# The running inverse of a triangular solver: from SBUF into two PSUM banks, with the priorities of two stages set anew

## The chip, the cores and the metric

The kernel runs on one core of a Trainium2 chip. The metric is the time of one execution on the device, in microseconds; of a kernel that is timed, the median of its runs counts. Engines are called as in the profile: PE (matrix products), DVE, ACT, POOL (GpSimd) and SP (which issues the DMAs).

## The reference

Two layers of a diffusion backbone over 512 latent tokens and 256 context tokens, width 1024. Layer 0 joins a bidirectional gated delta rule (four heads of 128) with grouped-query attention; layer 1 is a Conformer convolution; a SwiGLU follows each. What matters here is the delta rule, worked in chunks of 64 tokens, and in it the triangular system of each chunk, head and direction:

```python
def gated_delta_chunked(q, k, v, g, beta, s0, need_out):
    ...
    decay = jnp.exp(jnp.where(incl, gcum[..., :, None] - gcum[..., None, :], -jnp.inf))
    kb = kc * bc
    lower = jnp.where(strict, jnp.einsum("nbhcd,nbhsd->nbhcs", kb, kc) * decay, 0.0)
    eye = jnp.eye(DELTA_CHUNK, dtype=F32)
    rhs = jnp.concatenate([vc * bc, kb * jnp.exp(gcum)[..., None]], axis=-1)
    sol = lax.linalg.triangular_solve(lower + eye, rhs, left_side=True, lower=True, unit_diagonal=True)
    u, w = sol[..., :dv], sol[..., dv:]
    ...

def bidirectional_delta(q, k, v, g, beta, s0_fwd, s0_bwd, need_out):
    o_f, s_f = gated_delta_chunked(q, k, v, g[:, :, 0], beta[:, :, 0], s0_fwd, need_out)
    rev = lambda t: jnp.flip(t, axis=1)
    o_b, s_b = gated_delta_chunked(rev(q), rev(k), rev(v), rev(g[:, :, 1]), rev(beta[:, :, 1]), s0_bwd, need_out)
```

The kernel doesn't solve against the right sides. It inverts the 32x32 blocks on the diagonal, and the next stage makes u and w from the inverses with matrix products.

## The kernel before

The work runs in four stages, each planned when the program is built: the inputs; the heads; delta rule with attention; and the tail (output projection, SwiGLU, Conformer, SwiGLU). A stage is a list of operations, each with one or more engines on which it may run and a cost for each ("ways"), with operations that it depends on, and with buffers that it takes and gives back. `Plan.run` (L62 to 124) sets them in order: again and again it takes, of all that are ready, the one with the least start time on its model, less a weight times the length of the path behind it plus a bias. The biases are tables by name, and by name and engine (`BIAS1` for the heads, `BIAS` for delta rule with attention, L134 and L135). So a table settles which engine does what and in which order each engine's instructions stand; on the chip each engine then works through its list in that order, waiting where an operand or a buffer isn't there.

The heads' stage (`plan_heads`, L590) runs until about 246 us. All 8 banks of PSUM are one pool there, "pp", of which an operation takes one bank.

- A convolution is made of matmuls in four parts (L204 to L206: three products for each of 8 blocks, as the fp32 inputs are split into a high and a low part, `whi` and `wlo`, the latter by L573 on DVE or GpSimd, from `weights`). Its bank `ps_in` is then read by taps (L653, DVE, tile `cv`), by turns for keys, values and queries.
- For attention queries, the rows of a product are normed (L956, `qn`) and turned by position ("rope": L573, tiles `qr`, `kkr`, `rt`).
- `solver(d)`, once for each of two directions (L1045 to L1100), loads the strictly lower blocks into `blk` and identity into `xi`: each has 32x32 elements on 96 partitions (four loads of 24) in SBUF, and comes from a pool "b4" of four. There are 31 steps j. `row_mul` (L1075) makes the outer product of the column of `blk` under the diagonal and the row j of `xi`, into `tm`; `row_sub` (L1079) takes it off the rows below. Each step has (31 - j)(j + 1) elements per partition, 31 at the ends, 256 in the middle, 5,456 in all. A step needs the one before, and all run on DVE; the two directions lie beside each other in its list, so that one fills the other's gaps. Then `turned` makes a transposed copy into `blk` (L564, ACT or GpSimd), and `x_out` (L1094) has four DMAs write `xi`, and four the transposed copy, to DRAM (`xblk`).
- `gate` (L1135 ff.) makes silu of a product on ACT (L1147, tile `zz`, a pool "dd" of two), times a gain on DVE or GpSimd (L573), and a DMA to DRAM (L1153, `zimg`).
- `keys64` turns keys (L1027) and makes `kst` of them (L564 and L1038). `query` sums squares on ACT (L1117, `junk`).

The next stage clears its tiles first (L1359, from `masks`, on ACT here; they are issued by the program's order behind ACT's last work of the stage before, or amid it) and loads the inverses: L1380, `xu<-xblk`. Its first DVE work is `qd<-qr`. All DMAs of these places stand in SP's one list: an issue that waits for its data holds up those behind it.

Of the kernel before, what the change touches and what calls it, by code (L numbers as in the profile page):

```python
# [151 lines left out]
def kernel(ctx: ExitStack, tc: tile.TileContext, I: dict, out: bass.AP, dbg=None):  # L152
    nc = tc.nc
    V, S, G, E, SP = nc.vector, nc.scalar, nc.gpsimd, nc.tensor, nc.sync
# [11 lines left out]
    def bc(ap, axis, shape):  # L166
        return ap.unsqueeze(axis).to_broadcast(shape)
# [134 lines left out]
    with ExitStack() as st:  # L302
# [10 lines left out]
        def copy_on(e, dst, src):  # L313
            {"ACT": S.copy, "DVE": V.tensor_copy, "Pool": G.tensor_copy}[e](dst, src)
# [262 lines left out]
    pp = pool(p1, "pp", 8, space=PSUM)  # L577
# [11 lines left out]
    def bank(n, *shape):  # L589
        return pp.tile([P] + list(shape), F32, tag="pp", name=n)  # L590

    def plan_heads(op):
# [3 lines left out]
        def after(*names):  # L596
            return tuple(last[n] for n in names if n in last)
# [175 lines left out]
        a = op({"DVE": 0.25}, g13, (a,))  # L773
# [274 lines left out]
        def solver(d):  # L1048
            s = {}

            def ld_blk():
                s["blk"] = pj.tile([96, 32, 32], F32, tag="b4", name="blk", bufs=4)
                for b in range(4):
                    src = nimg[d][32 * b : 32 * b + 32, :, :, 32 * b : 32 * b + 32].rearrange("r c h q -> (c h) r q")
                    SP.dma_start(s["blk"][b * NB : (b + 1) * NB], src)

            def ld_eye():
                s["xi"] = pj.tile([96, 32, 32], F32, tag="b4", name="xi", bufs=4)
                SP.dma_start(s["xi"].rearrange("p r q -> p (r q)"), I["eye32"].partition_broadcast(96))

            a = op({"SP": 2.2}, ld_blk, nst[d], seq=after("b4"), lat=DLAT, take=("b4",))
            b = op({"SP": 1.1}, ld_eye, (), seq=(a,), lat=DLAT, take=("b4",))
            a = op({}, None, (a, b))
            for j in range(31):
                m = 31 - j

                def step(j=j, m=m):
                    t = {}

                    def row_mul():  # L1070
                        blk, xi = s["blk"], s["xi"]
# [3 lines left out]
                        V.tensor_tensor(t["tv"], bc(col, 2, (96, m, j + 1)), bc(xi[:, j, : j + 1], 1, (96, m, j + 1)), ALU.mult)  # L1075

                    def row_sub():
                        xi = s["xi"]
                        V.tensor_tensor(xi[:, j + 1 :, : j + 1], xi[:, j + 1 :, : j + 1], t["tv"], ALU.subtract)  # L1079

                    return row_mul, row_sub

                for f in step():
                    a = op({"DVE": 0.07 + m * (j + 1) / 960.0}, f, (a,))

            def turned(e):
                s["xj"] = s["blk"]
                copy_on(e, s["xj"], s["xi"].rearrange("p r q -> p q r"))

            def x_out(w):  # L1090
                def f():
                    t_ = s["xi"] if w == d else s["xj"]
                    for b in range(4):
                        SP.dma_start(xblk[d][w, 32 * b : 32 * b + 32].rearrange("r c h q -> (c h) r q"), t_[b * NB : (b + 1) * NB])  # L1094
# [1368 lines left out]
```

## Time and profile before

| what | value |
|---|---|
| median of 3 runs | 1409.06 us (1408.97 to 1411.34) |
| the profiled execution: its own time | 1409.85 us |
| its span | 1408.1 us |
| mean granted clock of PE | 0.973 |
| busy: PE, DVE, ACT, POOL | 1339.5 (95%), 870.8 (62%), 477.1 (34%), 233.2 us (17%) |
| heads' stage before the solver, 60 to 158.5 us | PE 90.16, DVE 87.80, ACT 55.47, POOL 66.82 |
| delta rule with attention, 246.6 to 412 us | PE 162.09, DVE 141.32 of 165.4 |

The times in the rows are those of one execution, from its span's start. Busy time is what an engine spent on instructions, and the share is that of the whole span; in a window, it is read against the window's length. In the timeline, rows of one kind that follow one another are one row with a count (x2); its length runs from the first one's start to the last one's end, and neighbours overlap by some 0.06 us, since an instruction starts before the one ahead of it has drained.

### The profile page before, as it was taken

The numbers are of one execution on the slowest core, as the hardware profiler recorded it, in microseconds if no ns is written. First come the engines' busy times: TensorE is split into PE (matmuls) and PEld (weight loads), VectorE is DVE, ScalarE is ACT, GpSimd is POOL, SyncE is SP. The second block draws the span as 40 slices with busy tenths as digits, with TensorE's granted clock in tenths as the row PEclk, the third lists the DMA queues.
The fourth block names the chain that finished last, engine by engine and source line by source line (L and its number), as shares of the span: only waits on it lengthen the run. The fifth ranks groups of instructions, "written<-read, shape, count | busy, mean of one in ns | idle before, by whom it ended". The sixth has DMA issues, their size and how long they took to land.

```text
span 1408.1 us, 19059 instructions
## 1 busy us (share of the span) xinstructions
PE 1339.5 (95%) x7267; PEld 1125.3 (80%) x7267; DVE 870.8 (62%) x1634; ACT 477.1 (34%) x1003; POOL 233.2 (17%) x272
## 2 busy tenths in 40 slices
PE   6999986999999999999999989997999999999998
PEld 4888876788978988888888768886788888888886
DVE  3689898789886765565578636549574333343233
ACT  6656533577652411111100145112442122222221
POOL 2667464211010200000000201214040000000000
PEclk9999998699999999999999989998999999999999
DMA  8345724554237355554668603110313232233221
GB/s 318 132 130 167 172 83 78 142 183 143 67 122 239 111 186 166 186 165 150 207 225 269 205 32 120 61 46 16 104 61 103 78 120 88 92 109 116 90 94 71
DMA packets 105851, 184.74 MB, mean 131 GB/s; under 512 B 33731, under 2 KB 50450, under 8 KB 105760
## 3 DMA queue, kind: packets, MB, share of 16 engines
q1 hardware_dynamic: 105760, 183.53, 40.8%
q8 instruction: 57, 0.93, 0.3%
q14 instruction: 34, 0.28, 0.1%
HBM read 172.44 MB, written 11.06 MB: 130 GB/s over the span
## 4 chain that ended last, share of the span: by engine, by line
PE 79%; DVE 13%; DMA 3%; issue 1%; ACT 1%; SPq 1%; POOL 1%; DVEq 0%; POOLq 0%; ACTq 0%
PE ps_in L206 12%; PE ps_in L204 12%; PE ps_in L205 12%; PE ps_y L1740 7%; PE ps_y L1741 7%; PE ps_y L1742 7%; DVE cv L653 2%; PE ps_in L2094 2%; PE ps_in L2092 2%; PE ps_in L2093 2%; DVE tm L1075 2%; PE ps_pt L1288 1%; DVE xi L1079 1%; PE ps_pv L1310 1%; PE ps_sc L1258 1%
## 5 line engine op out<-in xcount | busy, mean ns | idle before, releaser
L206 PE MATMUL ps_in<-ah,wlo 128*128 128x512 f32 (+1 forms) x768 | 285.5, 372 | 1.1 <-DVE wlo L573 0.8
L204 PE MATMUL ps_in<-ah,whi 128*128 128x512 f32 (+1 forms) x768 | 285.6, 372 | 0.0
L205 PE MATMUL ps_in<-al,whi 128*128 128x512 f32 (+1 forms) x768 | 285.2, 371 | 0.0
L573 DVE TENSOR_TENSOR wlo<-wraw,whi 128x1024 fp32r<-128x1024 f32 x164 | 204.2, 1254 | 129.0 <-ACT whi L564 123.3
L206 PEld LDWEIGHTS ps_in<-ah,wlo 128*128 128x128 f32 x768 | 144.6, 188 | 26.8 <-DVE wlo L573 1.7
L204 PEld LDWEIGHTS ps_in<-ah,whi 128*128 128x128 f32 x768 | 144.7, 188 | 25.1 <-DVE whi L564 0.2
L205 PEld LDWEIGHTS ps_in<-al,whi 128*128 128x128 f32 x768 | 144.7, 188 | 24.9
L564 ACT CAST whi<-wraw 128x1024 fp32r<-128x1024 f32 x92 | 96.3, 1050 | 164.6 <-PE ps_y L1741 79.9
L1740 PE MATMUL ps_y<-whi,hh 128*128 128x512 f32 x352 | 138.8, 394 | 0.0
L1742 PE MATMUL ps_y<-wlo,hh 128*128 128x512 f32 x352 | 138.2, 393 | 0.0
L1741 PE MATMUL ps_y<-whi,hl 128*128 128x512 f32 x352 | 138.1, 392 | 0.0
L564 DVE CAST whi<-wraw 128x1024 fp32r<-128x1024 f32 x70 | 48.6, 694 | 141.8 <-PE ps_in L205 106.9
L1945 ACT ACTIVATE sg<-ps_in 128x512 f32<-128x512 f32 x44 | 26.3, 599 | 290.7 <-PE ps_in L206 290.5
L1607 DVE CUSTOM_DVE_ANT_0 wada<-wada,csrow 128x1024 f32<-128x1024 f32 x80 | 96.7, 1220 | 13.6 <-DMA wada<-in_wmB 13.3
L180 POOL TENSOR_TENSOR rr<-rr,mhalf 128x1 f32<-128x1 f32 x28 | 16.0, 573 | 488.8 <-DVE rr L1779 457.3
L1740 PEld LDWEIGHTS ps_y<-whi,hh 128*128 128x128 f32 x352 | 66.5, 189 | 15.9 <-issue 1.5
L1741 PEld LDWEIGHTS ps_y<-whi,hl 128*128 128x128 f32 x352 | 66.6, 189 | 14.5
L1742 PEld LDWEIGHTS ps_y<-wlo,hh 128*128 128x128 f32 x352 | 66.5, 189 | 14.6
L1948 DVE TENSOR_TENSOR sg<-sg,ps_in 128x512 f32<-128x512 f32 x44 | 30.0, 684 | 63.6 <-PE ps_in L206 63.6
L573 POOL TENSOR_TENSOR matsl<-fraw,matsh 128x512 fp32r<-128x512 f32 x5 | 8.2, 1670 | 322.7 <-ACT matsh L564 322.7
L1761 ACT ACTIVATE junk<-ps_y 128x512 bf16<-128x512 f32 x32 | 19.1, 598 | 122.7 <-PE ps_y L1742 110.9
L653 DVE SCALAR_TENSOR_TENSOR cv<-ps_in,convw,cv 128x510 f32<-128x510 f32 (+3 forms) x80 | 48.9, 635 | 2.7 <-ACT cv L568 1.7
(382 smaller groups left out, 2635.8 us busy)
## 6 DMA issues: line engine op xcount, KB each, us to landing
wraw<-in_wfin SPq DMA_DIRECT2D x88, 512.0 KB
wada<-in_wmB SPq DMA_DIRECT2D x80, 512.0 KB
wraw<-in_wfout SPq DMA_DIRECT2D x44, 512.0 KB
mraw<-in_wmA SPq DMA_DIRECT2D x16, 512.0 KB
wraw<-in_wcin SPq DMA_DIRECT2D x16, 512.0 KB
wraw<-in_wqkv SPq DMA_DIRECT2D x12, 512.0 KB
wraw<-in_wcout SPq DMA_DIRECT2D x8, 512.0 KB
rw<-grow SPq DMA_DIRECT2D x8, 384.0 KB
```

The source lines that it names most:

```text
L204: E.matmul(ps, wh, xh, start=start, stop=False)
L205: E.matmul(ps, wh, xl, start=False, stop=False)
L206: E.matmul(ps, wl, xh, start=False, stop=stop)
L564: {"ACT": S.copy, "DVE": V.tensor_copy, "Pool": G.tensor_copy}[e](dst, src)
L573: {"DVE": V, "Pool": G}[e].tensor_tensor(dst, a, b, o)
L653: V.scalar_tensor_tensor(s["cv"][:, o], s["ps"][:, i], convw[:, ft, j : j + 1], s["cv"][:, o], op0=ALU.mult, op1=ALU.add)
L1075: V.tensor_tensor(t["tv"], bc(col, 2, (96, m, j + 1)), bc(xi[:, j, : j + 1], 1, (96, m, j + 1)), ALU.mult)
L1607: V.tensor_tensor_reduce(s["raw"], s["raw"], csrow[0], 1.0, 0.0, ALU.mult, ALU.add, accs[:, part, j : j + 1])
L1740: E.matmul(acc[t], ah[:, ts_], wh[:, o], start=i == 0 and j == 0, stop=False)
L1741: E.matmul(acc[t], al[:, ts_], wh[:, o], start=False, stop=False)
L1742: E.matmul(acc[t], ah[:, ts_], wl[:, o], start=False, stop=end)
L1948: V.tensor_tensor(s["g"], s["g"], pss[1]["ps"], ALU.mult)
```

## The change

The solver's running inverse is kept in two banks of PSUM, of 16 rows of 32 each. A new operation `x_init` copies the identity from `xi` into them, on ACT or DVE, and takes both banks of "pp" for the solver's whole length. `row_mul` reads its row there; `row_sub` works on the rows of each bank in an instruction of its own, so that the first 15 steps have two of them. At the end `turned` makes the transposed copy from PSUM in two halves on ACT or DVE (no longer GpSimd), a new operation `straight` copies the banks back into `xi`, and then the banks are given back. Both tables are set anew: all 97 values of `BIAS1` (and seven new names), and 166 of the 174 of `BIAS`.

```diff
-BIAS1, TW1 = {'centre': 773, 'decays': 8173, 'g1': 51842, 'g10': 84141,
...
+BIAS1, TW1 = {'centre': -1101, 'decays': 92262, 'g1': 7769, 'g10': 130739,
...
+            def x_init(e):
+
+                s["x"] = [bank("ps_x", 16, 32)[:96] for n in range(2)]
+                for n in range(2):
+                    copy_on(e, s["x"][n], s["xi"][:, 16 * n : 16 * n + 16])
+
             a = op({"SP": 2.2}, ld_blk, nst[d], seq=after("b4"), lat=DLAT, take=("b4",))
             b = op({"SP": 1.1}, ld_eye, (), seq=(a,), lat=DLAT, take=("b4",))
+            b = op({"ACT": 1.0, "DVE": 1.2}, x_init, (b,), seq=(a,), take=("pp", "pp"))
             a = op({}, None, (a, b))
             for j in range(31):
...
                     def row_mul():
-                        blk, xi = s["blk"], s["xi"]
+                        blk, xi = s["blk"], s["x"][j // 16]
...
-                        V.tensor_tensor(t["tv"], bc(col, 2, (96, m, j + 1)), bc(xi[:, j, : j + 1], 1, (96, m, j + 1)), ALU.mult)
+                        V.tensor_tensor(t["tv"], bc(col, 2, (96, m, j + 1)), bc(xi[:, j % 16, : j + 1], 1, (96, m, j + 1)), ALU.mult)
 
                     def row_sub():
-                        xi = s["xi"]
-                        V.tensor_tensor(xi[:, j + 1 :, : j + 1], xi[:, j + 1 :, : j + 1], t["tv"], ALU.subtract)
+                        for n in range(2):
+                            lo, hi = max(j + 1, 16 * n), 16 * n + 16
+                            if lo < hi:
+                                x = s["x"][n][:, lo - 16 * n :, : j + 1]
+                                V.tensor_tensor(x, x, t["tv"][:, lo - j - 1 : hi - j - 1], ALU.subtract)
...
             def turned(e):
                 s["xj"] = s["blk"]
-                copy_on(e, s["xj"], s["xi"].rearrange("p r q -> p q r"))
+                for n in range(2):
+                    copy_on(e, s["xj"][:, :, 16 * n : 16 * n + 16], s["x"][n].rearrange("p r q -> p q r"))
+
+            def straight(e):
+                for n in range(2):
+                    copy_on(e, s["xi"][:, 16 * n : 16 * n + 16], s["x"][n])
...
-            b = op({"ACT": 0.95, "Pool": 3.5}, turned, (a,))
+            b = op({"ACT": 1.15, "DVE": 1.25}, turned, (a,))
+            a = op({"ACT": 1.15, "DVE": 1.25}, straight, (a,))
+            op({}, None, (a, b), rel=("pp", "pp"))
             op({"SP": 2.2}, x_out(d), (a,), lat=DLAT)
             op({"SP": 2.2}, x_out(1 - d), (b,), lat=DLAT)
```

What the tables and the new costs make of the order is read from the two programs. The counts first: in the heads' stage DVE has 62 products and 92 subtractions of the solver, where it had 62 and 62; the four transposing copies `blk<-ps_x` are on DVE, where two stood on GpSimd; the four copies `ps_x<-xi` and the four `xi<-ps_x` are on ACT. Six casts of `kst` and two copies of keys go from DVE to ACT; of the products for position, six of `qr`, two of `kkr` and sixteen of `rt` go from DVE to GpSimd, so do two of `zz` and one addition of a mask. In the stage behind, few engines change, and places by a row or two.

DVE's list in the middle of the solver, where both directions run (`tm` the outer product, `blk` the loaded blocks, `xi` the inverse); before:

```order
L1075 TENSOR_TENSOR tm<-blk,xi 96x207
L1075 TENSOR_TENSOR tm<-blk,xi 96x256
L1079 TENSOR_TENSOR xi<-xi,tm 96x23x9
L1079 TENSOR_TENSOR xi<-xi,tm 96x16x16
L1075 TENSOR_TENSOR tm<-blk,xi 96x220
L1075 TENSOR_TENSOR tm<-blk,xi 96x255
L1079 TENSOR_TENSOR xi<-xi,tm 96x22x10
L1079 TENSOR_TENSOR xi<-xi,tm 96x15x17
```

and now (`ps_x` is a bank with half of the inverse's rows):

```order
L1082 TENSOR_TENSOR tm<-blk,ps_x 96x207
L1082 TENSOR_TENSOR tm<-blk,ps_x 96x255
L1089 TENSOR_TENSOR ps_x<-ps_x,tm 96x7x9
L1089 TENSOR_TENSOR ps_x<-ps_x,tm 96x16x9
L1089 TENSOR_TENSOR ps_x<-ps_x,tm 96x15
L1089 TENSOR_TENSOR ps_x<-ps_x,tm 96x16x15
L1082 TENSOR_TENSOR tm<-blk,ps_x 96x220
L1082 TENSOR_TENSOR tm<-blk,ps_x 96x256
L1089 TENSOR_TENSOR ps_x<-ps_x,tm 96x6x10
L1089 TENSOR_TENSOR ps_x<-ps_x,tm 96x16x10
L1089 TENSOR_TENSOR ps_x<-ps_x,tm 96x16x16
```

The 23 rows of one subtraction have become 7 in the one bank and 16 in the other; the directions still take turns.

SP's list at the end of the stage: the DMAs that write the inverses (`xblk`) and the gate (`zimg`), up to the first load of the next stage (`xu`); before:

```order
L1094 DMA xblk0_86<-xi_1883 24x32x32 x4
L1153 DMA zimg_90<-zz_2699 128x256
L1153 DMA zimg_90<-zz_2710 128x256
L1094 DMA xblk1_87<-xi_1986 24x32x32 x4
L1094 DMA xblk0_86<-blk_1878 24x32x32 x4
L1153 DMA zimg_90<-zz_2790 128x256
L1153 DMA zimg_90<-zz_2794 128x256
L1094 DMA xblk1_87<-blk_1981 24x32x32 x4
L1380 DMA xu_2976<-xblk0_86 128x2x128
```

and now:

```order
L1110 DMA xblk0_86<-xi_1894 24x32x32 x4
L1171 DMA zimg_90<-zz_2764 128x256
L1171 DMA zimg_90<-zz_2775 128x256
L1110 DMA xblk0_86<-blk_1889 24x32x32 x4
L1110 DMA xblk1_87<-xi_1937 24x32x32 x4
L1171 DMA zimg_90<-zz_2838 128x256
L1171 DMA zimg_90<-zz_2842 128x256
L1110 DMA xblk1_87<-blk_1932 24x32x32 x4
L1398 DMA xu_3014<-xblk0_86 128x2x128
```

The first direction's transposed copy now goes ahead of the second direction's inverse; the last two `zimg` and the four DMAs behind them keep their places at the end.

ACT's list behind the last step of the solver (`kst` the turned keys, `masks` what the next stage's tiles are cleared with, `zz` the gate); before, from the clearings on:

```order
L1359 ACTIVATE u_2933<-masks 128x512
L1359 ACTIVATE u_2934<-masks 128x512
L1359 ACTIVATE w_2935<-masks 128x256
L1359 ACTIVATE w_2936<-masks 128x256
L1359 ACTIVATE x_2937<-masks 128x256
L1359 ACTIVATE x_2938<-masks 128x256
L1359 ACTIVATE u_2943<-masks 128x512
L1147 ACTIVATE zz<-ps_z 128x256 x2
L1117 ACTIVATE junk,sq__669<-ps_qtok 128x128 x16
```

and now:

```order
L564 COPY xi<-ps_x 96x512
L564 CAST kst<-ps_kt 128x2x128 x6
L1377 ACTIVATE u_2977<-masks 128x512
L1377 ACTIVATE u_2978<-masks 128x512
L1377 ACTIVATE w_2979<-masks 128x256
L1377 ACTIVATE w_2980<-masks 128x256
L1377 ACTIVATE x_2982<-masks 128x256
L1377 ACTIVATE w_2986<-masks 128x256
L1377 ACTIVATE u_2988<-masks 128x512
L1165 ACTIVATE zz<-ps_z 128x256 x2
```

A copy of the inverse's half and six casts now stand ahead of the clearings and of the last two `zz`.

More of the change, by code (lines that the diff above doesn't have):

```diff
@@ new lines @@
+BIAS1, TW1 = {'centre': -1101, 'decays': 92262, 'g1': 7769, 'g10': 130739, 'g11': 26781, 'g12': -4062, 'g13': 79204, 'g14': 249349, 'g2': 17342, 'g3': 1285, 'g4': 194307, 'g5': 37439, 'g6': 1491, 'g7': 970, 'g8': 474, 'g9': 259395, 'h_add': 1594, 'h_cos': -15926, 'h_gain': 815, 'h_norm': 80085, 'h_root': -5581, 'h_sin': 79195, 'h_sq': -2774, 'h_sum': 52156, 'k_gram': 16915, 'k_high': -7712, 'k_low': 86865, 'k_norm': -1648, 'k_out': 12660, 'k_sq': -129, 'k_t': 834, 'k_tc': -13125, 'kd': -91914, 'kt': -8334, 'ld_blk': 56961, 'ld_eye': 57598, 'ld_rw': -7458, 'ld_w': -2654, 'lower': -283, 'masked': -2759, 'mm_in': 527, 'mm_ps_qb': -81, 'mm_ps_z': -2194, 'n_out': 779, 'q_sq': 207239, 'q_tok': -41985, 'qk': -88015, 'qk_dm': -161959, 'rk_eps': 118562, 'rk_root': -1668, 'row_mul': 2996, 'row_sub': 2940, 'silu': -8400, 'sq_eps': -213745, 'straight': -62046, 't_ps_ktok': 1005, 't_ps_vtok': 11168, 'tanh': 69661, 'tap': 2976, 'times': 97, 'turned': -132629, 'v_copy': -11671, 'v_out': 165807, 'w_high': 747, 'w_low': 656, 'x_init': -43111, 'x_out': -33907, 'z_norm': 75430, 'z_out': -28509, 'z_silu': 133352, ('centre', 'ACT'): -573, ('centre', 'DVE'): 806, ('h_add', 'DVE'): -9700, ('h_add', 'Pool'): -18762, ('h_cos', 'DVE'): 89525, ('h_cos', 'Pool'): 80270, ('h_gain', 'DVE'): -21028, ('h_gain', 'Pool'): -17691, ('h_sin', 'DVE'): -57254, ('h_sin', 'Pool'): 45597, ('k_high', 'ACT'): 93829, ('k_high', 'DVE'): -156804, ('k_norm', 'ACT'): -2262, ('k_norm', 'DVE'): -2137, ('k_tc', 'ACT'): 7911, ('k_tc', 'DVE'): -40120, ('kd', 'ACT'): 462, ('kd', 'DVE'): 31654, ('kd', 'Pool'): 84908, ('masked', 'DVE'): -91068, ('masked', 'Pool'): -6414, ('straight', 'ACT'): 133854, ('straight', 'DVE'): 29856, ('turned', 'ACT'): -50929, ('turned', 'DVE'): 137147, ('v_copy', 'ACT'): 9811, ('v_copy', 'DVE'): -99219, ('w_low', 'DVE'): -3773, ('w_low', 'Pool'): -10532, ('x_init', 'ACT'): 47101, ('x_init', 'DVE'): 27310, ('z_norm', 'DVE'): 3022, ('z_norm', 'Pool'): 1788}, 0.000200
@@ L1074, in row_mul @@
                         t["tv"] = tm[:, : m * (j + 1)].rearrange("p (r q) -> p r q", q=j + 1)
-                        V.tensor_tensor(t["tv"], bc(col, 2, (96, m, j + 1)), bc(xi[:, j, : j + 1], 1, (96, m, j + 1)), ALU.mult)
+                        V.tensor_tensor(t["tv"], bc(col, 2, (96, m, j + 1)), bc(xi[:, j % 16, : j + 1], 1, (96, m, j + 1)), ALU.mult)
                     def row_sub():
-                        xi = s["xi"]
-                        V.tensor_tensor(xi[:, j + 1 :, : j + 1], xi[:, j + 1 :, : j + 1], t["tv"], ALU.subtract)
+                        for n in range(2):
[3 more added lines that the diff above has]
+                                V.tensor_tensor(x, x, t["tv"][:, lo - j - 1 : hi - j - 1], ALU.subtract)
                     return row_mul, row_sub
-                for f in step():
-                    a = op({"DVE": 0.07 + m * (j + 1) / 960.0}, f, (a,))
+                mul, sub = step()
+                a = op({"DVE": 0.07 + m * (j + 1) / 960.0}, mul, (a,))
+                a = op({"DVE": (0.14 if j < 15 else 0.07) + m * (j + 1) / 960.0}, sub, (a,))
             def turned(e):
                 s["xj"] = s["blk"]
-                copy_on(e, s["xj"], s["xi"].rearrange("p r q -> p q r"))
+                for n in range(2):
[3 more added lines that the diff above has]
+                    copy_on(e, s["xi"][:, 16 * n : 16 * n + 16], s["x"][n])
             def x_out(w):
```

3 lines of the change are left out of this document (1 added, 2 removed).

## Prediction

> **What bounds the kernel now.** The windows come first, cut at the places where the change works: the head stage up to the triangular solver's first step (60 to 158.5 us), the solver up to the end of its first direction (228.4; the second ends at 233.4), then attention with the delta rule (246.6 to 412). The tail follows. Columns: engine busy time with its instructions, granted TensorE clock, DMA share.
>
> ```profile
> core 0: us, PE busy (x) PEld busy (x) DVE busy (x) ACT busy (x) POOL busy (x), PEclk, DMA share, GB/s
> 60.00:158.50 98.50, 90.16 (x586) 80.86 (x586) 87.80 (x196) 55.47 (x162) 66.82 (x72) 0.98 0.52 144
> 158.50:228.40 69.90, 56.30 (x336) 50.41 (x335) 69.09 (x161) 21.14 (x36) 38.15 (x28) 0.90 0.33 93
> 246.60:412.00 165.40, 162.09 (x1424) 140.15 (x1424) 141.32 (x369) 111.05 (x288) 23.89 (x59) 0.94 0.42 127
> ```
>
> While the solver runs, DVE is busy 69.09 of 69.90 us: there it is the bound, and PE waits for it. From 246.6 us on PE is busy 98% of the time, so what the solver's stage gains or loses should pass whole to the end. The groups of DVE within 158.5 to 233.4 us say what it does (busy us, mean ns, idle before).
>
> ```profile
> L1075 DVE TENSOR_TENSOR tm<-blk,xi 96x31 f32<-96x31 f32 (+15 forms) x62 | 28.5, 484 | 2.6 <-issue 2.3
> L1079 DVE TENSOR_TENSOR xi<-xi,tm 96x31 f32<-96x31 f32 (+15 forms) x62 | 21.7, 378 | 0.3
> L653 DVE SCALAR_TENSOR_TENSOR cv<-ps_in,convw,cv 128x510 f32<-128x510 f32 (+3 forms) x32 | 19.9, 669 | 0.0
> L573 DVE TENSOR_TENSOR zz<-zz,onorm 128x256 f32<-128x256 f32 x6 | 5.2, 880 | 1.9 <-ACT zz L1147 1.9
> L573 DVE TENSOR_TENSOR qr<-qn,rope 128x256 f32<-128x256 f32 x3 | 1.2, 412 | 0.0
> ```
>
> Both solver lines process the same elements, yet one is 6.8 us dearer; and zz takes 880 ns where qr, as large, takes 412. The timeline shows why: DVE above, GpSimd (POOL) in the same stretches below.
>
> ```profile
> 179.38 2.07 DVE L1075 TENSOR_TENSOR tm<-blk,xi 96x156 f32<-96x156 f32 x1
> 181.37 2.59 DVE L1079 TENSOR_TENSOR xi<-xi,tm 96x240 f32<-96x240 f32 x1
> ...
> 186.98 2.88 DVE L1075 TENSOR_TENSOR tm<-blk,xi 96x192 f32<-96x192 f32 x2
> ...
> 190.39 2.91 DVE L1075 TENSOR_TENSOR tm<-blk,xi 96x207 f32<-96x207 f32 x2
> ```
>
> ```profile
> 178.89 4.81 POOL L573 TENSOR_TENSOR wlo<-wraw,whi 128x1024 fp32r<-128x1024 f32 x2
> ...
> 186.90 2.41 POOL L573 TENSOR_TENSOR wlo<-wraw,whi 128x1024 fp32r<-128x1024 f32 x1 [0.70 <-ACT whi L609]
> ```
>
> The DVE instruction at 181.37 ends at 183.96, just after GpSimd's pair of wlo (183.70), the one at 186.98 after the wlo of 186.90 to 189.31. A step that should take 0.3 to 0.4 us waits out a GpSimd instruction. The taps, which read one operand from PSUM, do not; they come between two rows of the solver, and zz, all in SBUF, does:
>
> ```profile
> 214.04 3.36 DVE L573 TENSOR_TENSOR zz<-zz,onorm 128x256 f32<-128x256 f32 x2
> 217.32 4.02 DVE L653 SCALAR_TENSOR_TENSOR cv<-ps_in,convw,cv 128x511 f32<-128x511 f32 x6
> ```
>
> ```profile
> 205.53 8.24 POOL L573 TENSOR_TENSOR kkr<-kkr,rt 128x128 f32<-128x128 f32 x1 [4.35 <-DVE kkr L573]
> 213.73 0.90 POOL L573 TENSOR_TENSOR qr<-qr,rt 128x256 f32<-128x256 f32 x1
> 214.60 5.01 POOL L573 TENSOR_TENSOR wlo<-wraw,whi 128x1024 fp32r<-128x1024 f32 x2
> ```
>
> Six taps take 4.02 us under wlo, 0.66 each; and a GpSimd row of half a microsecond lasted 8.24 us during the solver's unbroken run. So the two engines shut each other out, when both operands of DVE lie in SBUF.
>
> **The change, part by part.** Undisturbed rows of DVE give the prices (the time from one start to the next is what an instruction costs in a queue, its duration what one costs that the next waits for):
>
> ```profile
> 198.96 4.68 DVE L653 SCALAR_TENSOR_TENSOR cv<-ps_in,convw,cv 128x510 f32<-128x510 f32 x7
> 203.56 0.72 DVE L1079 TENSOR_TENSOR xi<-xi,tm 96x240 f32<-96x240 f32 x2
> ...
> 207.97 0.71 DVE L1075 TENSOR_TENSOR tm<-blk,xi 96x220 f32<-96x220 f32 x2
> ...
> 212.83 0.62 DVE L1075 TENSOR_TENSOR tm<-blk,xi 96x156 f32<-96x156 f32 x2
> ...
> 232.78 0.22 DVE L1079 TENSOR_TENSOR xi<-xi,tm 96x60 f32<-96x60 f32 x1
> 233.03 0.19 DVE L1075 TENSOR_TENSOR tm<-blk,xi 96x31 f32<-96x31 f32 x1
> ```
>
> *Stalls.* With the inverse in PSUM, each solver instruction has one operand in SBUF, like the taps. The four DVE rows above hold 10.45 us for six instructions; at 0.15 us plus 1.04 ns an element (0.19 us for 31 elements, 0.22 for 60) they need about 2.1. That is 8.3 us; shorter ones of the same kind I put at 2.7, since the two groups' means make 62 x (0.484 + 0.378) = 53.4 us where 124 instructions by 0.15 plus 21,824 elements by 1.04 ns make 41.3, some 12 less. Taken: -11, between -8 and -12. [...]
>
> *PSUM's price.* Durations alone would say it is nothing (the taps' mean of 669 ns for 510 elements is 0.15 plus 1.04 ns each, 0.68). The distance from start to start says otherwise. From 207.97 to 212.83 stand 16 solver instructions of both directions, 3,608 elements: 4.86 us less 3.75 is 0.07 each. Seven taps from PSUM take 4.60 us, 0.657 each, less 0.53 for 510 elements: 0.125. Now 124 instructions become 154, since each of the first 15 steps subtracts in two banks. 154 x 0.125 is 19.3, against 124 x 0.07 = 8.7. Where one direction runs alone each step waits for the last (0.19 in the final row): 26 such instructions before by 0.12 more (3.1), 23 after by an estimated 0.1 (2.3). Sum +9.8. No row writes PSUM from DVE: if it is free the price is SBUF's (154 x 0.07, sum about +2), if it costs the same 0.055 again on the 92 subtractions, +15. The middle is nearest to the taps. [...]
>
> *Other DVE work in the window.* Three rope products of qr and one of kkr go to GpSimd (-1.2), two of the window's six zz too or later (-0.7); the zz stall at 214.04 goes (-2.6), a new one is likely (+1); of the idle 1.9 before zz I take 1 back; the transposing copies of the first direction come in (2 x 0.6: +1.2). GpSimd's added products and zz lie in its free half of the window (38.15 of 69.9 busy, 7.8 of that the wait in kkr).
>
> Window: -11 + 9.8 - 1.2 - 0.7 - 2.6 + 1 - 1 + 1.2 = -4.5.
>
> *Start.* Today DVE waits for the loads:
>
> ```profile
> 158.53 0.19 DVE L1075 TENSOR_TENSOR tm<-blk,xi 96x31 f32<-96x31 f32 x1 [2.31 <-issue]
> ```
>
> The copy into PSUM now stands between load and first step: one bank of 512 elements on ACT, by its 512-element rows below (0.57) +0.7 with the hand-over. The taps queued behind it on ACT need DVE, which is waiting too. Before the solver DVE loses rope products, a mask addition and two copies, some 3 us; half lies on loads, so -1.5, between -4 and +2, as GpSimd takes the mask addition.
>
> *End.* The GpSimd transposition that goes was hidden: SP reached its DMAs only at 241.55.
>
> ```profile
> 239.31 2.15 SPq L1153 DMA_DIRECT2D zimg<-zz  x2
> 241.55 2.79 SPq L1094 DMA_DIRECT2D xblk<-blk  x4
> ```
>
> ```profile
> 230.88 1.33 ACT L1359 ACTIVATE m<-masks 128x256 f32<-128x256 f32 x4
> 232.11 1.14 ACT L1359 ACTIVATE u<-masks 128x512 f32<-128x512 f32 x2
> ```
>
> ```profile
> 246.63 0.36 DVE L564 COPY qd<-qr 128x128 f32<-128x128 f32 x2 [2.05 <-DMA xblk<-blk]
> ```
>
> Attention starts when the last xblk lands, 13.2 us after the solver's end. In the new order ACT, after that end, has half of straight (0.6), six casts of kst (2 to 2.6, with DVE's halves between), seven clearings (3 x 0.57 + 4 x 0.33 = 3.0), and only then the last two zz (256 elements too, 0.7): some 6.7 us. SP's last zimg wait for these, and behind them the last four xblk: 6.7 + 0.35 (zz on DVE) + 1.4 (two DMAs, half of the four in 2.79) + 2.8 + 2.3 (from 244.34 to the copy at 246.63), 13.5, or 14.3 with the slower casts. So +1, between -1 and +3.
>
> Attention's new order changes places by one or two rows and a few engines: 0, give or take 1.
>
> Sum: -4.5 + 0.7 - 1.5 + 1 = -4.3. The profiled execution took 1409.85, so 1405.5; the median of the runs lies 0.8 lower: **1404.7 us**.
>
> **The rivals.** *PSUM is as cheap as SBUF* (for it the equal durations, against it the start distances): 7.7 us less, 1397. *A wash*: the stage hangs on what was hidden, loads before the solver and SP's queue at the end, so that a shorter window only waits longer; 1409. For it: DVE idles at 158.53 and 246.63 behind DMAs; against it: between them it hardly idles. *Slower, by banks*: the solver holds four of eight PSUM banks. PE already queues for banks that taps free (us waited, times, longest):
>
> ```profile
> PE ps_kt L1027 <- DVE cv L653: 8.8, 3, 8.4
> ```
>
> ```profile
> 169.75:173.63 3.88, 3.88 (x19) 3.20 (x18) 3.88 (x12) 2.68 (x5) 1.67 (x1) 1.00 0.67 224
> ```
>
> In this stretch, where the matmuls of two convolutions run, 19 take 3.88 us, 0.204 each, so a pair (48 matmuls) takes 9.8 us. If pairs can't overlap with the taps of the last, DVE waits for its taps. It decides against the change from 4.3 us of DVE waits on; half of one pair at two places gives 9.8, less 4.3: +5.5, 1414.6. Against it: DVE never waited for PE here, and 13 us of solver steps stand between the last two groups of taps. *The change doing nothing* needs stalls with PSUM operands; the taps under wlo exclude it.
>
> **How the numbers follow.** Forecast (1401 to 1408) 0.50, cheap PSUM 0.13, wash 0.22, banks 0.15. The range, 1398 to 1412, leaves out half of the first and most of the last rival. About 0.2% (2.8 us) is what a measurement of this kernel tells from no change. Faster: three quarters of the forecast, all of cheap PSUM and a little of the wash, 0.54; same: 0.30; slower: 0.16.
>
> **What would show it.** Solver instructions never over 0.6 us under GpSimd; subtractions about 0.125 us plus elements apart; first step near 158, last near 229, first attention copy near 242. Wrong if DVE idles behind PE in the solver (banks), if GpSimd still stretches its rows, or if SP stands at zimg for over 8 us after the solver's end.

## The result, and the profile after

The changed kernel takes 1391.97 us, the median of 4 runs (1390.09 to 1393.60); before, beside it, 1409.96 (4 runs). The ratio is 0.9874, with a 95% interval of 0.9853 to 0.9896: 18 us less, where 4.4 were forecast and the range went down to 1398.

The profiled executions are 1409.85 us before and 1390.09 after, spans 1408.1 and 1388.3. Cut at the same events, the 19.8 us between them lie here (before; after):

| stretch | before | after | difference |
|---|---|---|---|
| start to the solver's first step | 158.53 | 158.65 | +0.1 |
| the solver, first step to the end of its last | 74.9 | 60.3 | -14.6 |
| to the next stage's first copy of `qd` | 13.2 | 13.1 | -0.1 |
| to its first `ps_mix` near its end (407.1; 387.9) | 160.5 | 155.8 | -4.7 |
| the rest | 1001.0 | 1000.4 | -0.6 |

The windows of the changed kernel, cut there (columns as before):

```profile
core 0: us, PE busy (x) PEld busy (x) DVE busy (x) ACT busy (x) POOL busy (x), PEclk, DMA share, GB/s
60.00:158.65 98.65, 92.38 (x590) 82.52 (x590) 83.82 (x187) 57.41 (x166) 75.27 (x97) 0.98 0.51 142
158.65:218.92 60.27, 58.40 (x392) 53.18 (x390) 58.43 (x199) 26.91 (x49) 29.05 (x26) 1.00 0.43 116
232.07:387.90 155.83, 153.81 (x1385) 134.39 (x1386) 136.61 (x356) 108.24 (x282) 26.15 (x63) 0.96 0.42 127
```

In the solver DVE is as full as it was (58.43 of 60.27 us), and now PE is too (58.40). The groups of DVE in that window:

```profile
L1089 DVE TENSOR_TENSOR ps_x<-ps_x,tm 96x60 f32<-96x60 f32 (+20 forms) x92 | 20.6, 272 | 0.4
L653 DVE SCALAR_TENSOR_TENSOR cv<-ps_in,convw,cv 128x510 f32<-128x510 f32 (+3 forms) x32 | 19.9, 665 | 0.0
L1082 DVE TENSOR_TENSOR tm<-blk,ps_x 96x31 f32<-96x31 f32 (+15 forms) x62 | 18.2, 322 | 3.8 <-ACT ps_x L564 3.5
L564 DVE COPY blk<-ps_x 96x512 f32<-96x512 f32 x3 | 2.0, 683 | 0.1
L573 DVE TENSOR_TENSOR zz<-zz,onorm 128x256 f32<-128x256 f32 x4 | 1.7, 421 | 0.8 <-ACT zz L1165 0.8
L949 DVE TENSOR_SCALAR ssh<-ssh 128x4 f32<-128x4 f32 x2 | 1.3, 630 | 0.1
```

The two solver groups hold 38.8 us, where they held 50.2, though there are 154 instructions instead of 124. The product's mean is 322 ns, it was 484. `zz` is at 421 ns, it was 880. The timeline shows DVE in the 4.7 us in which GpSimd makes two `wlo`, the kind of place at which DVE stood still before:

```profile
178.69 0.61 DVE L1082 TENSOR_TENSOR tm<-blk,ps_x 96x156 f32<-96x156 f32 x2
179.23 0.75 DVE L1089 TENSOR_TENSOR ps_x<-ps_x,tm 96x60 f32<-96x60 f32 x4
179.90 0.64 DVE L1082 TENSOR_TENSOR tm<-blk,ps_x 96x175 f32<-96x175 f32 x2
```

```profile
178.26 4.74 POOL L573 TENSOR_TENSOR wlo<-wraw,whi 128x1024 fp32r<-128x1024 f32 x2
```

Nothing is stretched on either side. In the whole solver eight `wlo` of GpSimd lie beside 154 instructions, of which none takes over 0.5 us (the longest 0.41); before, 12 of 124 did, with 16.4 us. Then what an instruction costs: from the first of these rows to the last there are 14 solver instructions of both directions, 3,161 elements (a row names the size of its first instruction; the other direction's is smaller).

```profile
198.09 0.69 DVE L1082 TENSOR_TENSOR tm<-blk,ps_x 96x255 f32<-96x255 f32 x2
198.71 0.70 DVE L1089 TENSOR_TENSOR ps_x<-ps_x,tm 96x255 f32<-96x255 f32 x2
...
202.28 0.40 DVE L1089 TENSOR_TENSOR ps_x<-ps_x,tm 96x240 f32<-96x240 f32 x1
```

4.19 us, less 3.29 for the elements at 1.04 ns, is 0.064 us each. (The 1.04 ns are the prediction's; from these, 0.299 us apart at a mean of 226 elements, to the eight `dm` of 512 in the kernel before, 0.599 us apart, from 239.62 us, the distance grows by 1.05 ns an element.) The prediction had 0.125 for PSUM, and 0.07 for SBUF. (The expectations of e8 and e12 below take 0.04 to 0.05 us for this spacing; the rows give 0.064.) Where DVE starts the solver, and the end of the stage on SP's queue:

```profile
158.65 0.18 DVE L1082 TENSOR_TENSOR tm<-blk,ps_x 96x31 f32<-96x31 f32 x1 [3.18 <-ACT ps_x L564]
```

```profile
226.17 1.21 SPq L1171 DMA_DIRECT2D zimg<-zz  x2
227.42 2.92 SPq L1110 DMA_DIRECT2D xblk<-blk  x4
```

The last inverses are issued 8.5 us after the solver's end, as before (8.1), and the first copy of `qd` follows at 232.07, 13.1 us after it. PE's waits from 158.5 to 248 us:

```profile
PE ps_qt L1248 <- DVE qd L564: 5.2, 2, 5.0
PE ps_in L204 <- DVE cv L653: 1.4, 2, 0.9
```

For banks that taps free PE waits 1.4 us in all, and DVE never waits for PE in the solver.

### The profile page after: what moved, and what is told of

Its sections match the earlier page's. It is cut to its first block, busy times and chain, and to the rows that moved or that the text cites. A ratio compares the mean times of both kernels' runs of the same rounds, so it can differ in the third digit from the quotient of the medians.

```text
span 1388.3 us, 19096 instructions
## 1 busy us (share of the span) xinstructions
PE 1335.3 (96%) x7267; PEld 1121.0 (81%) x7267; DVE 847.8 (61%) x1631; ACT 484.3 (35%) x1019; POOL 229.2 (17%) x299
## 4 chain that ended last, share of the span: by engine, by line
PE 82%; DVE 8%; DMA 4%; POOL 2%; ACT 2%; issue 1%; SPq 1%; DVEq 0%; POOLq 0%; ACTq 0%
PE ps_in L204 12%; PE ps_in L206 12%; PE ps_in L205 12%; PE ps_y L1758 7%; PE ps_y L1759 7%; PE ps_y L1760 7%; PE ps_in L2112 2%; PE ps_in L2110 2%; PE ps_in L2111 2%; PE ps_pt L1306 1%; PE ps_pv L1328 1%; PE ps_o L1369 1%; PE ps_sc L1276 1%; PE ps_du L1369 1%; PE ps_a L1830 1%
## 5 line engine op out<-in xcount | busy, mean ns | idle before, releaser
L1625 DVE CUSTOM_DVE_ANT_0 wada<-wada,csrow 128x1024 f32<-128x1024 f32 x80 | 96.7, 1222 | 12.4 <-DMA wada<-in_wmB 12.0
L1760 PEld LDWEIGHTS ps_y<-wlo,hh 128*128 128x128 f32 x352 | 66.6, 189 | 14.6
L2110 PE MATMUL ps_in<-whi,ah 128*128 128x512 f32 x128 | 50.0, 391 | 0.0
```

The source lines that it names most:

```text
L1625: V.tensor_tensor_reduce(s["raw"], s["raw"], csrow[0], 1.0, 0.0, ALU.mult, ALU.add, accs[:, part, j : j + 1])
L1760: E.matmul(acc[t], ah[:, ts_], wl[:, o], start=False, stop=end)
L2110: E.matmul(acc[t], k["h"][:, tk], wh[:, o], start=False, stop=False)
```

## The experiments

Theory A is the place: in SBUF a solver instruction waits for GpSimd, in PSUM it doesn't, and PSUM costs nothing. Theory B is the order: the new tables moved work off DVE. A third question came from the table above: what the next stage gained.

**e1: the same order, the inverse in SBUF.**

```diff
-                s["x"] = [bank("ps_x", 16, 32)[:96] for n in range(2)]
+                s["x"] = [s["xi"][:, 16 * n : 16 * n + 16] for n in range(2)]
```

> The changed kernel with every instruction in its place on every engine, except that the two halves of the inverse are the two halves of xi in SBUF (the copies in and out copy xi onto itself). Theory A (the place: with two operands in SBUF a DVE instruction waits for GpSimd; in PSUM it doesn't and pays nothing for it): the solver takes 11 to 15 us longer again, about 72 to 75 us from its first to its last step, rows of 2 to 3 us come back in it, and the kernel takes about 1404 us. Theory B (the order: the new tables moved work from DVE to GpSimd and ACT, and that is the gain): the solver stays at about 60 us and the kernel at about 1392.

1404.03 us (4 runs), ratio 0.9951 (0.9933 to 0.9969). The solver's window, and DVE and GpSimd in it:

```profile
158.30:231.90 73.60, 62.34 (x403) 55.43 (x402) 69.01 (x199) 27.05 (x52) 44.05 (x30) 0.98 0.35 95
```

```profile
170.50 2.78 DVE L1089 TENSOR_TENSOR xi<-xi,tm 96x28 f32<-96x28 f32 x4
...
200.98 3.55 DVE L1089 TENSOR_TENSOR xi<-xi,tm 96x48 f32<-96x48 f32 x3
```

```profile
170.54 2.36 POOL L573 TENSOR_TENSOR wlo<-wraw,whi 128x1024 fp32r<-128x1024 f32 x1
...
200.99 2.44 POOL L573 TENSOR_TENSOR wlo<-wraw,whi 128x1024 fp32r<-128x1024 f32 x1
```

Instructions of 28 elements are under way for as long as GpSimd's `wlo` beside them. Six solver instructions take over 0.5 us, 12.2 us in all. With every instruction in its place, the memory alone makes 13.3 us in the solver and 12.1 us of the time. The other 6 us of the gain come with the rest of the change (the new order, the copies, the subtractions in two), which helps in SBUF too; where they lie was not taken apart.

**e2: the changed code with both tables of before; e9: the same, with the new operations' biases taken from the changed table; e4: the kernel before with both new tables.** In each, the two table lines (`BIAS1`, `BIAS`) are those of the other kernel, and in e9:

```diff
-BIAS1, TW1 = {... of before ...}
+BIAS1, TW1 = {... of before, and x_init, straight, turned of the changed table ...}
```

> The changed kernel's code with both tables of before (the new operations then have no bias). Theory A: the solver's instructions have no rows over 0.6 us and hold some 39 us instead of 50; what the tables add is small, so about 1396 us, if the old table doesn't place the new operations badly. Theory B: about 1408.

> As e2 (the changed code with the tables of before), but the operations that hold or free the two banks (copy in, copies out) have the biases of the changed table. In e2 the transposed copies came 43 us after the solver's last step, so its four banks were held until then, and PE waited. Theory A with banks as the reason for e2's loss: the banks come free right behind the solver, the gap from its end to the first copy of qd falls from 52 us to under 20, and the time to about 1400. If the old table is bad for another reason (it sends the gate behind the solver in any case): the gap stays over 30 us and the time over 1415.

> The kernel before with both new tables (the inverse in SBUF, the old operations). Theory A: the stalls stay, the tables give at most the 4.6 us of the next stage and about 3 us of moved work: about 1402 us, the solver about 72 us. Theory B: most of the gain, about 1395 us, the solver near 62.

All three are slower than before: e2 1437.01 us, ratio 1.019 (1.0174 to 1.0207); e9 1424.65 (2 runs), 1.0124 (1.008 to 1.0168); e4 1417.61, 1.0052 (1.0035 to 1.0068). Both theories missed. The solver itself is as theory A has it: 64.5 us in e2 and 58 in e9, in PSUM, and 70.8 in e4, in SBUF. What is lost comes behind it: first step of the next stage 52 us after the solver in e2, 43 in e9, 30 in e4. SP's queue there, of e2, then e9, then e4:

```profile
239.08 19.99 SPq L1171 DMA_DIRECT2D zimg<-zz  x7
```

```profile
227.97 14.84 SPq L1171 DMA_DIRECT2D zimg<-zz  x2
```

```profile
230.37 20.32 SPq L1153 DMA_DIRECT2D zimg<-zz  x8
```

In these orders the gate, most of which both kernels lay under the solver, comes behind it. In e2 it starts late as well, since PE stands at the keys for the `kst` that DVE has behind the solver:

```profile
PE ps_kt L1027 <- DVE kst L1038: 15.0, 2, 14.7
```

Free banks are at most a part of what e2 lacked: in e9 they are free within 4 us of the solver's end, the ratio is 0.7% lower, and a gap of 43 us remains. So a table is worth something only with the operations it was made for, and neither half of the change can be had alone with the other kernel's table.

**e3: the changed kernel with before's table for the next stage (`BIAS`) alone.**

> The changed kernel with before's table for delta rule with attention alone; the heads' stage is the changed one. The trace shows this stage 4.6 us shorter after the change (first copy of qd to the first ps_mix: 160.5 us before, 155.8 after). If the new table does that: about 1396.5 us and 160 us there. If it comes from something else (the clock granted, the times at which loads land): about 1392 and 156.

1391.98 us, the changed kernel's median to 0.01; the stage took 156.7 us in the profiled execution. That table does nothing that can be measured.

**e5 and e6: e1 and the changed kernel, both without GpSimd's fourteen `wlo`.**

```diff
             def w_low(e):
+                if e == "Pool":
+                    s["l"] = s["h"]
+                    return
```

> As e1 (the inverse in SBUF, the order of the changed kernel), but the fourteen subtractions wlo that GpSimd makes in the heads' stage are left out; the matmuls read whi in their place, so the low part of those weights is missing in the result. If it is GpSimd's work that stretches DVE's rows: no solver row over 0.8 us but for the short GpSimd products that are left, the solver near 61 us as in the changed kernel instead of 73.5. If SBUF as such is slow for the solver, it stays at 70 or more.

> The changed kernel with the same fourteen subtractions of GpSimd left out (the low part of those weights is missing in the result). With the inverse in PSUM GpSimd doesn't touch the solver: the solver stays within 1 us of 60.3, the time within 2 us of 1392. If GpSimd slows it in PSUM too, it falls by over 2 us.

1386.90 and 1385.07 us (2 runs each). The solver's windows, of e5 and of e6:

```profile
151.80:213.00 61.20, 58.52 (x398) 53.67 (x398) 59.39 (x198) 27.12 (x51) 20.33 (x21) 1.00 0.41 113
```

```profile
148.90:209.00 60.10, 58.39 (x393) 53.29 (x392) 57.76 (x199) 26.65 (x50) 10.04 (x18) 1.00 0.43 117
```

In SBUF the solver falls from 73.6 to 61.2 us when GpSimd's `wlo` are gone, in PSUM from 60.3 to 60.1. That is theory A, from both sides. The 1.1 us between the two are too little to read: the changed kernel's solver, unaltered, took 60.3, 61.2, 60.1, 60.6 and 62.0 us in five profiled executions (after, e3, e10, e13, e14). They show that PSUM costs no more than some 2 us in the whole solver. The time of e6 does fall by 7 us against the changed kernel, more than the 2 allowed: its solver starts at 148.9 instead of 158.65. Ahead of it, too, DVE has rows with two operands in SBUF, and they are shorter without `wlo` (the eight `ks<-th,cv`: 584 ns in the mean, 1014 in the changed kernel); the rest of the earlier start was not taken apart.

**e7: the inverse in SBUF, the product in PSUM.**

```diff
-                s["x"] = [bank("ps_x", 16, 32)[:96] for n in range(2)]
+                s["x"] = [s["xi"][:, 16 * n : 16 * n + 16] for n in range(2)]
+                s["tm"] = [bank("ps_x", 512)[:96] for n in range(2)][0]
...
-                        tm = pj.tile([96, 256], F32, tag=f"tm{d}", name="tm", bufs=1)
+                        tm = s["tm"]
```

> The order of the changed kernel; the inverse in SBUF as in e1, but the product tm in one of the two banks. Now a subtraction has one operand in SBUF (xi) and one in PSUM (tm); a product has two in SBUF (blk, xi) and writes PSUM. If it is two operands read from SBUF that make the wait: products are stretched (rows of 1 to 2.6 us), subtractions are not, and the solver lies between, about 66 us, the time about 1398. If it is the place of the result, or of the inverse: subtractions are stretched as in e1 (some 8 us in all), and products not.

1402.40 us, the solver 73.5. Durations are shortest/median/longest in ns, with first and last start:

```profile
L1083 DVE TENSOR_TENSOR ps_x<-blk,xi x62: 183/376/2608, 156.2 to 229.1; 96x31 f32<-96x31 f32 x4, 96x60 f32<-96x60 f32 x4, 96x87 f32<-96x87 f32 x4, 96x112 f32<-96x112 f32 x4
```

```profile
L1090 DVE TENSOR_TENSOR xi<-xi,ps_x x92: 157/240/411, 156.4 to 229.5; 96x48 f32<-96x48 f32 x6, 96x60 f32<-96x60 f32 x6, 96x15 f32<-96x15 f32 x4, 96x28 f32<-96x28 f32 x4
```

The product reads two operands in SBUF and is stretched to 2.6 us; the subtraction reads one in SBUF and one in PSUM, writes SBUF, and never exceeds 0.41. So it is the two operands read that count, not the place of the result. But the guess of half the loss was wrong. With half of the instructions exposed nothing was saved: here 11 products take over 0.5 us, 17.7 us in all, where e1 had two products and four subtractions, with eight `wlo` beside the solver in both. A `wlo` that meets no subtraction seems to meet the next product.

**e12: e5 with one subtraction per step, 124 instructions instead of 154.**

```diff
-                        for n in range(2):
...
+                        x = s["xi"][:, j + 1 :, : j + 1]
+                        V.tensor_tensor(x, x, t["tv"], ALU.subtract)
```

> As e5 (inverse in SBUF, the order of the changed kernel, GpSimd's wlo left out, so the low part of those weights is missing in the result), but a subtraction is one instruction, as before the change: 124 solver instructions instead of 154. The solver took 61.2 us in e5. If an instruction more costs 0.125 us, as predicted: 57.5 us; by 0.04: 60.

1384.67 us (2 runs); the solver:

```profile
148.80:208.60 59.80, 58.20 (x396) 53.28 (x395) 57.68 (x168) 26.41 (x48) 10.98 (x19) 1.00 0.41 115
```

1.4 us less for 30 instructions, about the 60 of the second case and not the 57.5 of the first. The difference is no larger than what one and the same solver varies by (60.1 to 62.0 us above), so it only bounds the price of the additional instructions; at 0.07 us each, the prediction's spacing in SBUF, 30 would be 2.1 us.

**e8, e15, e16: the price of more instructions.** Each subtraction is cut once more by rows, 88 more: e8 in PSUM, e15 in SBUF (on e5), e16 in PSUM with the cuts of the first 15 steps taken from the two banks by turns.

```diff
+                                mid = (lo + hi) // 2
+                                for l, h in ((lo, mid), (mid, hi)):
...
+                                        V.tensor_tensor(x, x, t["tv"][:, l - j - 1 : h - j - 1], ALU.subtract)
```

> The changed kernel with each subtraction cut once more by rows: 88 subtractions more, the same elements. The prediction put the price of one more instruction with PSUM at 0.125 us: +11 us, about 1403. By the spacing seen after the change (0.04 to 0.05 us beside the elements) it is +4, about 1396.

> As e5 (inverse in SBUF, GpSimd's wlo left out, so the low part of those weights is missing in the result), with each subtraction cut once more as in e8: 88 more. In e8 they cost 0.17 us each, in e12 against e5 an instruction of the solver cost 0.05. If two subtractions in a row on one bank of PSUM wait for each other: in SBUF they don't, the solver takes 61.2 + 4 = 65.5 us. If any subtraction right behind one of its own direction waits, or a short one has a floor: about 76 us, as in e8.

> As e8, but the four subtractions of one of the first 15 steps alternate between the banks (first half of the one, first half of the other, second halves); from step 15 on there is one bank, as in e8. If a bank is what waits: the steps up to 14, whose cuts are about two thirds of the 88, lose most of their cost, and the solver takes 64 to 68 us instead of 75.3. If not: 75 us again.

1405.60 us (10 runs), 1389.60 (2) and 1402.08 (4); the solver takes 75.3, 67.6 and 70.1 us. For each of the three, one step of eight cuts and one of four, each with the row behind it, whose start shows when the group was through; e8:

```profile
186.61 1.59 DVE L1092 TENSOR_TENSOR ps_x<-ps_x,tm 96x32 f32<-96x32 f32 x8
188.11 0.69 DVE L1082 TENSOR_TENSOR tm<-blk,ps_x 96x207 f32<-96x207 f32 x2
...
206.83 1.12 DVE L1092 TENSOR_TENSOR ps_x<-ps_x,tm 96x128 f32<-96x128 f32 x4
207.86 0.70 DVE L1082 TENSOR_TENSOR tm<-blk,ps_x 96x255 f32<-96x255 f32 x2
```

e16:

```profile
184.01 1.16 DVE L1092 TENSOR_TENSOR ps_x<-ps_x,tm 96x32 f32<-96x32 f32 x8
185.08 0.69 DVE L1082 TENSOR_TENSOR tm<-blk,ps_x 96x207 f32<-96x207 f32 x2
...
202.85 1.12 DVE L1092 TENSOR_TENSOR ps_x<-ps_x,tm 96x128 f32<-96x128 f32 x4
203.88 0.70 DVE L1082 TENSOR_TENSOR tm<-blk,ps_x 96x255 f32<-96x255 f32 x2
```

e15:

```profile
176.22 1.09 DVE L1095 TENSOR_TENSOR xi<-xi,tm 96x32 f32<-96x32 f32 x8
177.23 0.69 DVE L1085 TENSOR_TENSOR tm<-blk,xi 96x207 f32<-96x207 f32 x2
...
193.69 0.85 DVE L1095 TENSOR_TENSOR xi<-xi,tm 96x128 f32<-96x128 f32 x4
194.47 0.70 DVE L1085 TENSOR_TENSOR tm<-blk,xi 96x255 f32<-96x255 f32 x2
```

Eight cuts (a row names the size of the first) take 1.50 us where neighbours work on one bank (e8), 1.07 where they alternate (e16), 1.01 in SBUF (e15). The four of one bank take 1.03 in both PSUM kernels and 0.78 in SBUF: 0.125 us for each of the two pairs. All 88 cost 15.0 us in e8, 9.8 in e16 and 6.4 in e15; 88 by 0.07 are 6.2. So a cut on the same bank as the one right ahead waits for it; with another bank's cut between, or in SBUF, no wait shows. e8 missed both of its expected figures; e15 came nearer its first case (67.6 us, for 65.5), e16 fell between its two (70.1, for at most 68 or 75).

The traces also say what makes the wait. Each instruction there carries the semaphore that it waits for. Of the 88 second cuts, all 88 carry such a wait in e8 and in e16, and two in e15; in e8 86 of them start only after the end of the instruction ahead, in e16 the 30 of the steps with one bank. So the program as built holds a wait for two instructions on one bank of PSUM. Whether the hardware would need it, no run shows.

**e11, e10, e14, e13: PE's clock behind the stage.** e10 is the changed kernel, e11 the kernel before, with unread matmuls in the wait ahead of the next stage; e13 and e14 are the changed kernel and e10 once more, with e11 on one chip.

```diff
         plan.run()
+        warm = bank("ps_w", 512)
+        for i in range(22):
+            E.matmul(warm, aL[0][:, 0, :P], aL[0][:, 0, :], start=i == 0, stop=i == 21)
```

> The changed kernel, with 22 matmuls of 512 columns behind PE's last work in the heads' stage, whose result nobody reads: they fill the 5 us for which PE waits for the inverses. The rows show PE's clock at 0.50 from 231.9 to 245.3 us after that wait, and from 244 to 268 before the change. If the wait is what lowers the clock: it stays at 1.00, the next stage takes some 150 us instead of 155.8, and the kernel about 1386 us. If the low clock comes from the work behind (PE is busy there, but with small matmuls): no change, 1392, or 1 us more for the matmuls.

> The kernel before with the same 22 unread matmuls of 512 columns behind PE's last work in the heads' stage. Before the change PE's clock is at 0.50 from 244 to 268 us, longer than after it (13.4 us), and the next stage takes 160.5 us where the changed kernel takes 155.8 and e10 153.8. If the clock is what the changed kernel gained there: this stage falls to about 154 us, the kernel by about 6 us. If not: it stays over 158, and the matmuls cost 0 to 2 us.

> The changed kernel once more, beside e11 and e14 on one chip: a ratio of 0.987 to before; the next stage at 155 to 157 us.

> e10 once more, beside the changed kernel. If the clock is worth what the stage shows (153.8 against 155.8 us): 2 us less than the changed kernel. If the difference was chance: the same as the changed kernel within 0.5 us.

The ratios to before are 0.9868 (0.9831 to 0.9904) for e10, 0.987 (0.9848 to 0.9891) for e14, 0.9878 (0.9858 to 0.9897) for e13, and 0.9993 (0.9977 to 1.0009) for e11: no difference to the kernel without the matmuls in either case. (Of e14's two cases neither came: 1391.79 us, 0.8 less than e13.) The next stage's windows, from the first copy of `qd` to the first `ps_mix`, in the profiled executions of before, e13, e14, e11 and e10:

```profile
246.60:407.10 160.50, 157.26 (x1384) 136.84 (x1385) 136.57 (x360) 107.98 (x282) 23.39 (x59) 0.93 0.41 123
```

```profile
229.00:387.80 158.80, 156.55 (x1384) 136.49 (x1385) 136.64 (x356) 108.21 (x282) 26.08 (x63) 0.94 0.41 124
```

```profile
232.60:391.60 159.00, 156.41 (x1387) 136.49 (x1386) 136.82 (x356) 108.42 (x282) 26.43 (x63) 0.95 0.42 125
```

```profile
246.30:400.40 154.10, 151.03 (x1386) 132.12 (x1385) 135.82 (x360) 107.82 (x282) 23.44 (x59) 0.99 0.44 128
```

```profile
230.20:384.00 153.80, 149.53 (x1387) 131.12 (x1386) 136.66 (x356) 108.31 (x282) 26.81 (x63) 1.00 0.42 128
```

The stage's length goes with the clock, from 153.8 us at 1.00 to 160.5 at 0.93, and not with the kernel: the changed kernel has 155.8 in one execution and 158.8 in the other, and e10 and e14, one program, 153.8 and 159.0. In e14 the clock fell in spite of the matmuls, in e11 it stayed at 0.99 in the mean; that execution of e11 is the fastest of its twelve (1403.84, up to 1414.13), so its 154.1 us are not the kernel's usual time there. e13 missed its 155 to 157 us. So the 4.7 us in the table above can't be put down to the change: the stage differs by as much between executions of one program. How much is left on the mean stays open: of before there is one profiled execution.

## Why the prediction missed

- **What bounds the kernel**: right. DVE bounds the solver's stretch, and what it gained there came through to the end; the start and the end of the stage moved by 0.1 us each.
- **Stalls (-11, and -2.6 at zz)**: right in mechanism and nearly in size. e1 against e5, where only GpSimd's `wlo` go, gives 12.4 us.
- **PSUM's price (+9.8)**: this is the step that failed, and with it the forecast. The 0.125 us were read from the taps, as what an operand in PSUM costs, and laid on all 154 instructions. In the changed kernel the solver's instructions are 0.064 us apart beside their elements, no more than in SBUF (0.07). By the prediction's own sum that is 154 x 0.064 = 9.9 against 8.7, less 0.8 where one direction runs alone: +0.4 instead of +9.8. The window then comes to -13.9, and -14.6 was measured.

Whose price the 0.125 us are, the profile of the kernel before shows already:

```profile
239.62 4.87 DVE L1126 TENSOR_TENSOR dm<-dm,ps_qk 128x512 f32<-128x512 f32 x8
244.41 0.16 DVE L1162 TENSOR_SCALAR sq__669<-sq__669 128x16 f32<-128x16 f32 x1
...
470.11 1.41 DVE L1790 SCALAR_TENSOR_TENSOR hres<-yg,rr,hres 128x512 f32<-128x512 f32 x2
471.44 1.21 DVE L573 TENSOR_TENSOR wlo<-wraw,whi 128x1024 fp32r<-128x1024 f32 x1
```

Eight `tensor_tensor`, the solver's kind, each with an operand in PSUM, take 4.79 us from start to start: 0.599 each, less 0.533 for 512 elements, 0.066. Two `scalar_tensor_tensor`, the taps' kind, with a scalar for each partition as in the taps but all in SBUF, take 1.33: 0.13 each beside the elements. So the taps' 0.125 is the price of that kind of instruction, in SBUF too, and not of PSUM. Nor is it the wait of e8: the taps overlap (0.657 us apart, 0.73 long), and a single tap with an SBUF product behind it keeps the same distance (197.96 to 198.62 us). That both come to 0.125 is taken for chance.

- **Other DVE work and idle (-0.7, and -3.3 with the -2.6 at zz)**: near. The groups of the two windows give for `zz` -3.5 (six with 5.2 us, now four with 1.7; no new stall came), for the rope products of `qr` and `kkr` -1.5, for the transposing copies +2.0 and for two small scalings (`ssh`) +1.0, which the sum didn't have: -2.0, and the idle time within the window fell by another 0.8.
- **Start (+0.7 - 1.5)**: +0.1 in this execution. The copy into PSUM is waited for as said (3.18 us of idle before the first step, 2.31 before). The first step of the changed kernel lay at 158.65 in one execution and at 155.2 in the other (e13), so that the term can't be told from chance.
- **End (+1)**: the chain over ACT, `zz` and SP is there, and costs what the old one did, 13.1 us.
- **Next stage (0, give or take 1)**: the table does nothing (e3), as said. But the stage varies by 5 us between executions with PE's clock, which the prediction didn't know.
- **The rivals**: cheap PSUM was the case that came. It was given 0.13, with 1397, for the equal durations of rows that were there to read; against it stood a spacing that belonged to another kind of instruction. Its sum is stated as +2 where its terms make +1.3. Banks (PE's waits of 1.4 us) and the wash did not come. That the order could cost 27 us where it doesn't fit the code (e2) was in no rival.

With the price of the right row the forecast would have been 9.4 us lower, 1395.3. The other 3.3 us, down to the measured 1391.97, this sum doesn't explain: 0.7 of them are the window's, and the next stage's 4.7 lie between executions that differ by as much. The range began at 1398, and so left out most of the case that came.

## What to carry to other kernels

Where DVE's products of two SBUF operands last several times too long, look at what GpSimd does in the same stretch; one operand in PSUM ended it here (no solver row over 0.41 us, where the longest had taken 2.62), and exposing fewer instructions without removing the kind did not (e7). Where an accumulator in PSUM is worked on by several instructions in a row, let neighbours lie on different banks: the built program made one on the same bank wait (eight cuts took 1.50 us in e8 and 1.07 in e16, where neighbours alternate). The price of an instruction is to be taken from rows of the same kind of instruction, not from one that reads the same memory; and a list order from a tuned table is to be tried only with the code for which it was made.

## What the runs showed of the hardware

- On DVE a `tensor_tensor` with one operand in PSUM starts 0.064 to 0.066 us after the one ahead, beside the elements (the changed kernel from 198.09 us, before from 239.62), as with all operands in SBUF (0.07). The taps and `hres`, `scalar_tensor_tensor` with a scalar for each partition, take 0.125 to 0.13, from PSUM and from SBUF.
- A `tensor_tensor` of DVE with two operands in SBUF was held up beside a GpSimd `wlo` of 2.4 us, to 2.6 us (e1: four subtractions in 2.78 us beside the `wlo` at 170.54; e7: a product of 2.608 us); one with an operand in PSUM was not (at most 0.41 us, changed kernel and e7).
- In and after the wait of some 5 us ahead of the next stage PE's granted clock was 0.50, for 13.7 us in the changed kernel and for 23.9 before, though PE was busy most of that time: before, from 246.6 to 266.6 us, 18.09 of 20 us.

```profile
246.60:266.60 20.00, 18.09 (x94) 13.42 (x95) 12.94 (x36) 9.54 (x20) 5.53 (x17) 0.50 0.41 102
```

In the changed kernel the clock fell 4.3 us into the wait (PE idle from 227.4, 0.50 from 231.7) and was back at 1.00 at 245.3; before, it fell 1.9 us into it (241.9 and 243.8) and was back at 267.7. In e14 the clock fell to 0.50 at 235.8 us without such a wait: PE was busy for all of 224 to 232 us and for 3.04 of the next 4 us. What starts it there and what ends the low clock stay open.
